# Two passes of 256 tokens over the last four output tiles of a two-layer encoder, with weights split once

## The chip, the cores and the metric

The kernel runs on one core of a Trainium2 chip. The metric is device time in microseconds (us) of one execution; less is better. Engines are named as in the profile: PE (TensorE, matrix products; PEld is its weight loads), DVE (VectorE), ACT (ScalarE), POOL (GpSimd) and SP (SyncE, whose queue issues most DMA transfers).

## The reference

The program computes a two-layer encoder trunk over 1024 tokens of width 1024: layer 0 with global, windowed and memory attention, layer 1 with neighbourhood and memory attention, each with a gate and an output projection that is added to the residual, and a last RMS norm. Cut to what the change touches, the end of layer 1 and the last norm:

```python
y = jnp.concatenate([yc, ym], axis=-1) * jax.nn.silu(gate)      # (1, 1024, 1536)
x = x + y @ w_out_odd[o]                                         # (1, 1024, 1024)
...
return rmsnorm(x, final_norm_gain)   # x * rsqrt(mean(x*x) + 1e-6) * gain, per token
```

## The kernel before

The transposed residual is held as eight tiles of 128 features by 1024 tokens. The output projection is done by Strassen's method in Winograd's form on halves: features (four tiles and four tiles), tokens (512 and 512) and the inner dimension (768 and 768), so seven groups of products in place of eight. The four quarters of the result are c11, c12, c21, c22, each of four tiles of 128 x 512: c12 and c22 are the first 512 tokens in the order of the norm, "the earlier half" below, and c11 and c21 are the second 512 tokens, the ones that are ready last.

Each product of a group is a tile of 128 features: six blocks of 128 inner rows, and for every block three PE products (high weights by high activations, high by low, low by high), since a 32-bit float is split in two parts for the array. So a tile is 18 PE products. Weights come as two units of 384 columns per tile: a transfer into a raw buffer (tile name wraw, four buffers), a rounding copy on ACT that gives the high part (wh), and a subtraction that gives the low part (wl), on DVE and POOL in turn. The raw buffer is free again after the subtraction.

The order of the groups at the end of layer 1 (`out_project`, called with `last=True`): after the other quarters, group a12 adds to c11 (four tiles, PE banks pj, pj, s, s), with the norm of the earlier half worked in between: column sums of squares (line 283), the root, transposes that spread the root over the partitions (line 133), and the scaling and transfers out (lines 1900 to 1903). A fence holds a12's fourth tile back behind these transposes. The last group, a22, adds to c21. Its activations are the six tiles named H, its four output tiles are named yb.

Group a22 before: tiles 0, 1 and 2 with 512 columns each, in the banks of a12; the weights of tile 3 are split, and `finish` takes over. It works tile 3 in two passes of 256 tokens: after each pass comes the difference (DVE), its square (ACT), the sum of squares as one-column products with a vector of 1/1024 (line 1473, PE, into `ss`), the root (line 1480 and DVE), transposes, and the scaling of all eight tiles for these 256 tokens by DVE and POOL, with four transfers of 256 KB for each 256 tokens. Squares of six of the eight tiles are added by POOL to one total (tile vt); two are summed by PE on their own.

The scheduler of the framework sets the order of the rest by its own model of times; `issue_after` and `Pinned` hold some instructions in a written order. The named lines: 242 and 1334 products, 283 and 1473 sums, 133 transposes, 1359 `plus`, 1364 and 1366 squares and their adding, 1281 low parts of weights, 1518 the square of a difference, 1499 and 1501 POOL's scaling, 1496 transfers out. Instructions that go through `Pinned` carry line 62, those of `copy` line 125.

Of the kernel before, what the change touches and what calls it, by code (L numbers as in the profile page):

```python
# [10 lines left out]
F32R = mybir.dt.float32r  # L11
I32 = mybir.dt.int32
AF = mybir.ActivationFunctionType
OP = mybir.AluOpType
# [10 lines left out]
UNIT = 4  # L25
# [39 lines left out]
class Trunk:  # L65
# [1246 lines left out]
    def out_project(self, w, sd, yd, res, done, tags, banks, first, begun, last=False):  # L1312
# [4 lines left out]
        nc = self.nc  # L1317
        xb, yb = banks
        cut = [slice(u * 384, u * 384 + 384) for u in range(2)]

        def weights(i, kind, us=(0, 1)):

            src = sd[i][:, "3124".index(kind[1]), :] if kind[0] == "s" else w[i if kind[1] == "1" else 4 + i][:, 768 * (kind[2] == "2"):]
            for c in (cut[u] for u in us):
                with self.ahead("w"):
                    raw = self.st("wraw", [128, UNIT * 128], pool=self.base, bufs=4)[:, :384]
                    nc.sync.dma_start(raw, src[:, c])
                    yield self.w_parts(raw, self.either())
# [40 lines left out]
        apart = 7  # L1369
        c11, c22, c12, c21 = (self.halves(t) for t in tags["c"])  # L1370
        at = lambda c, i: c[i // 2][:, i % 2, :]
# [11 lines left out]
        y = self.y_parts(yd, tags["y"][1], "t1")  # L1383
# [7 lines left out]
        y = self.y_parts(yd, tags["y"][2], "t2")  # L1391
# [42 lines left out]
                square(x, i)  # L1434

        y = self.y_parts(yd, tags["y"][6], "t4", after)
        apart = 6 if last else 7
        for i in range(4):
            x = at(c21, i)
            if last and i == 3:  # L1440
                ws = list(weights(3, "a22"))
                break
            product(y, xb[i], weights(i, "a22"), True)
            with self.ahead("sink"):
                plus(x, xb[i], OP.subtract)
                square(x, 4 + i)
        if not last:
            list(done(c11 + c21, sums, 512, 512))
            return
        self.finish(c11 + c21, sums, [product, y, ws], at(c21, 3))  # L1450

    def finish(self, xs, sums, last, x3):

        nc, tc = self.nc, self.tc
        pinned = Pinned(tc, nc.vector)
        product, y, ws = last
        gains = [self.gain[:, 24 + kt:25 + kt] for kt in range(KT)]  # L1460
        at = [xs[k // 2][:, k % 2, :] for k in range(KT)]
        for k in range(7):
            if k < 3:
                nc.gpsimd.tensor_scalar(at[k], at[k], gains[k], 1.0, op0=OP.mult, op1=OP.mult)
            else:
                self.copy(at[k], at[k], gains[k])
        sq = self.st(self.square_tag, [128, 512])
        ss, rows = [self.ps("pv")[:, :16] for _ in range(2)], {}

        def sum_up(h, parts, start):  # L1470
            for i, a in enumerate(parts):
                for b, c in enumerate(range(cols[h].start, cols[h].stop, 128)):
                    self.last = nc.tensor.matmul(ss[h][:, b:b + 1], a[:, c:c + 128], self.inv_d, start=start and i + b == 0,
                                                 stop=not start, skip_group_check=True)

        def root(h):
            n = 2
            t = ss[h][:, 8:8 + n]
            r, y = (self.st(k, [128, n], pool=self.base, bufs=2) for k in ("rq_v", "rq_y"))
            nc.scalar.activation(t, ss[h][:, :n], AF.Sqrt, bias=self.eps)  # L1480
            pinned.reciprocal(r, t)
            yield
            pinned.scalar_tensor_tensor(t, ss[h][:, :n], EPS, r, op0=OP.add, op1=OP.mult)
            yield
            pinned.scalar_tensor_tensor(t, t, -0.5, r, op0=OP.mult, op1=OP.mult)
            yield
            pinned.scalar_tensor_tensor(y, t, 1.5, r, op0=OP.add, op1=OP.mult)
            yield
            rows[h] = [self.rows_of(y, n, k) for k in ("tr", "pj")]

        def scale(h):
            c = cols[h]
            sb = self.st("vt", [128, 512])[:, :c.stop - c.start]
            self.copy(sb, rows[h][1])
            two = lambda t: t[:, None, :].to_broadcast([128, 2, c.stop - c.start])
            out = lambda p: nc.sync.dma_start(
                self.io["out"][2 * p:2 * p + 2, :, 512 + c.start:512 + c.stop].rearrange("k p t -> p k t"), xs[p][:, :, c])
            x = xs[0][:, :, c]
            nc.gpsimd.tensor_tensor(x, x, two(sb), op=OP.mult)
            if h == 0:  # L1500
                nc.gpsimd.tensor_tensor(at[2][:, c], at[2][:, c], sb, op=OP.mult)
            for p in (2, 3):
                x = xs[p][:, :, c]
                pinned.tensor_tensor(x, x, two(rows[h][0]), op=OP.mult)
                yield
                out(p)
            if h == 0:
                pinned.tensor_tensor(at[3][:, c], at[3][:, c], rows[h][0], op=OP.mult)
            else:
                x = xs[1][:, :, c]  # L1510
                pinned.tensor_tensor(x, x, two(rows[h][0]), op=OP.mult)
            yield
            out(0)
            out(1)

        def difference(p, c):
            pinned.tensor_tensor(x3[:, c], x3[:, c], p, op=OP.subtract)
            nc.scalar.activation(sq[:, c], x3[:, c], AF.Square)
            self.copy(x3[:, c], x3[:, c], gains[7])
        cols = [slice(0, 256), slice(256, 512)]  # L1520
        p = self.ps("pj")[:, :256]
        product(y, p, ws, True, cols[0])
        difference(p, cols[0])
        p = self.ps("pj")[:, :256]
        end = product(y, p, ws, True, cols[1], range(2))
        with tc.issue_after(end.ins):
            sum_up(0, sums, True)
        with tc.issue_after(self.last.ins):
            end = product(y, p, ws, True, cols[1], range(2, 3))
        with tc.issue_after(end.ins):  # L1530
            sum_up(0, [sq], False)
        with tc.issue_after(self.last.ins):
            end = product(y, p, ws, True, cols[1], range(3, 6))
            sum_up(1, sums, True)
        first = root(0)
        for _ in range(4):
            next(first)
        difference(p, cols[1])
        with tc.issue_after(end.ins):
            list(first)  # L1540
        with tc.issue_after(self.turned.ins):
            sum_up(1, [sq], False)
        one = scale(0)
        next(one)
        next(one)
        list(root(1))
        list(one)
        list(scale(1))

    def front(self, w, pairs, order, values, plan, x1, squares, dests):  # L1550

# [675 lines left out]
```

## Time and profile before

| | |
|---|---|
| median of 3 runs | 1487.39 us (1487.01 to 1491.83) |
| the profiled execution, time | 1488.39 us |
| its span, first to last instruction | 1486.6 us |
| PE busy | 1465.6 us, 99% of the span |
| DVE, ACT, POOL busy | 70%, 56%, 43% |
| mean granted PE clock | 0.998 |
| chain that ended last | PE 85%, DMA 5%, DVE 4%, all else 6% |

The rows give the start of an instruction and its duration, both in us from the start of the span. PE products are pipelined: the listed duration of one (0.28 to 0.4 us) is longer than the distance to the next start, so that the price of a product is read from the distance of starts. In PE's rows a sum or a product that is built of several passes counts each of them (a one-column sum is two rows of PE).

### The profile page before, as it was taken

Reading aid. Unit: us, or ns where it says so; the run is one execution under the profiler, and the core shown is the slowest. Engines: PE = TensorE matmul, PEld = TensorE weight load, DVE = VectorE, ACT = ScalarE, POOL = GpSimd, SP = SyncE. Lnnn points to the kernel's source line nnn. Section 1 sums busy time; section 2 is a strip of 40 time slices with the busy share of each in tenths; the row PEclk is TensorE's granted clock in tenths of the full one; section 3 lists DMA queues with packets and bytes.
Section 4 is the critical chain, followed back from the end, with each engine's and each line's share of the span. In section 5 each row is a group of like instructions: output and inputs, shape, how many; then the busy total and the mean of one; then the engine's idle time right before and its main releaser. Section 6 shows DMA issues by size and latency. Waiting matters only on the chain.

```text
span 1486.6 us, 25518 instructions
## 1 busy us (share of the span) xinstructions
PE 1465.6 (99%) x8433; PEld 1275.1 (86%) x8433; DVE 1034.8 (70%) x2124; ACT 837.9 (56%) x1877; POOL 642.2 (43%) x767
## 2 busy tenths in 40 slices
PE   9899999999999999999999999999999999999998
PEld 8798888988888788888879887888998888888886
DVE  6687777777776578776687776654446787778674
ACT  7743665556655366655444444444446777777454
POOL 1223568556765656553450000001425556664454
PEclk9999999999999999999999999999999999999999
DMA  8966334334343524378553343567665568788834
GB/s 286 306 159 183 118 119 162 114 128 137 115 139 106 172 76 141 106 265 310 185 181 128 128 140 136 157 169 245 229 245 173 187 195 272 235 287 316 315 107 144
DMA packets 173860, 271.92 MB, mean 183 GB/s; under 512 B 15648, under 2 KB 96800, under 8 KB 172704
## 3 DMA queue, kind: packets, MB, share of 16 engines
q1 hardware_dynamic: 173296, 270.20, 56.2%
q8 instruction: 67, 1.10, 0.3%
q14 instruction: 65, 0.53, 0.1%
q10 hardware_dynamic: 432, 0.09, 0.0%
HBM read 174.28 MB, written 83.89 MB: 174 GB/s over the span
## 4 chain that ended last, share of the span: by engine, by line
PE 85%; DMA 5%; DVE 4%; issue 2%; ACT 2%; POOL 2%; SPq 0%; POOLq 0%; DVEq 0%; ACTq 0%
PE pj L242 15%; PE pj L62 11%; PE x L1619 7%; PE tr L133 6%; PE pv L1068 4%; PE y L1619 4%; PE pv L62 3%; PE s L62 3%; PE pj L1334 3%; PE tr L62 3%; PE sa L1334 2%; PE pv L1619 2%; PE sa L1035 2%; PE sa L1036 2%; PE s L1334 2%
## 5 line engine op out<-in xcount | busy, mean ns | idle before, releaser
L542 DVE TENSOR_TENSOR pl<-tr,ph 128x512 fp32r<-128x512 f32 (+2 forms) x352 | 204.1, 594 | 45.0 <-ACT ph L125 43.0
L242 PE MATMUL pj<-H,wh 128*128 128x512 f32 x704 | 233.7, 412 | 0.5 <-DVE vt L313 0.2
L125 ACT ACTIVATE ph<-tr 128x512 fp32r<-128x512 f32 (+2 forms) x352 | 176.3, 522 | 100.5 <-PE tr L133 76.4
L158 POOL TENSOR_SCALAR wh<-wraw 128x512 fp32r<-128x512 f32 x48 | 32.6, 682 | 275.9 <-PE x L1619 234.0
L125 ACT ACTIVATE wh<-wraw 128x384 fp32r<-128x384 f32 (+1 forms) x163 | 89.0, 553 | 99.4 <-DMA wraw<-w_mem 12.9
L242 PE MATMUL pj<-H,wl 128*128 128x512 f32 x352 | 139.1, 395 | 0.0
L242 PEld LDWEIGHTS pj<-H,wh 128*128 128x128 f32 x704 | 120.2, 189 | 18.3 <-POOL wh L158 1.1
L62 PE MATMUL pj<-H,wh 128*128 128x512 f32 x384 | 121.0, 396 | 0.0
L1121 POOL TENSOR_SCALAR pn<-pn,st 128x384 f32<-128x384 f32 (+1 forms) x128 | 72.4, 567 | 104.7 <-DVE st L1120 69.0
L133 PE MATMUL tr<-ident,P 128*128 128x128 f32 x752 | 115.4, 273 | 0.7 <-DVE pl L542 0.4
L1281 POOL TENSOR_TENSOR wl<-wraw,wh 128x384 fp32r<-128x384 f32 x56 | 63.2, 1130 | 91.4 <-ACT wh L125 85.6
L1119 ACT ACTIVATE pn<-pn,st 128x384 f32<-128x384 f32 (+1 forms) x128 | 75.1, 587 | 42.2 <-DVE st L1116 41.0
L133 PEld LDWEIGHTS tr<-ident,P 128*128 128x128 f32 x752 | 88.9, 140 | 9.1 <-DVE pl L542 1.4
L1041 ACT ACTIVATE P<-sa,st 128x1024 f32<-128x1024 f32 x64 | 71.5, 1117 | 35.3 <-PE tr L133 19.1
L1043 POOL TENSOR_SCALAR P<-P,st 128x1024 f32<-128x1024 f32 x64 | 74.0, 1159 | 32.3 <-DVE st L1042 32.3
L1040 DVE TENSOR_REDUCE st<-sa 128x1 f32<-128x1024 f32 x64 | 77.5, 1219 | 8.3 <-PE sa L1036 7.9
L62 PE MATMUL s<-k,q 128*128 128x384 f32 (+1 forms) x352 | 81.2, 327 | 0.0
L242 PEld LDWEIGHTS pj<-H,wl 128*128 128x128 f32 x352 | 66.2, 188 | 15.3
L62 PE MATMUL pj<-H,wl 128*128 128x512 f32 x192 | 75.6, 394 | 0.0
L160 POOL TENSOR_TENSOR wl<-wraw,wh 128x512 fp32r<-128x512 f32 x52 | 68.7, 1324 | 10.9 <-ACT wh L125 8.4
L62 PEld LDWEIGHTS pj<-H,wh 128*128 128x128 f32 x384 | 66.6, 188 | 5.4
L853 PE MATMUL pj<-ah,H 128*128 128x256 f32 x384 | 70.5, 281 | 0.0
(569 smaller groups left out, 4187.1 us busy)
## 6 DMA issues: line engine op xcount, KB each, us to landing
wraw<-w_o SPq DMA_DIRECT2D x52, 256.0 KB, 4.1
y<-yb SPq DMA_DIRECT2D x24, 512.0 KB, 3.2
wraw<-s SPq DMA_DIRECT2D x64, 192.0 KB, 3.7
wraw<-w_e SPq DMA_DIRECT2D x44, 256.0 KB, 3.2
k<-k SPq DMA_DIRECT2D x42, 256.0 KB, 5.4
s<-bias SPq DMA_DIRECT2D x56, 192.0 KB, 2.0
wq<-w_o SPq DMA_DIRECT2D x40, 256.0 KB, 3.4
y<-sg SPq DMA_DIRECT2D x18, 512.0 KB, 3.3
```

What stands on the lines that cost most here:

```text
L62: return lambda *a, **k: self.tc.keep_in_program_order(getattr(self.engine, name)(*a, **k))
L125: return self.nc.scalar.activation(out, in_, AF.Copy, scale=scale)
L133: self.turned = self.fence = self.pe.transpose(o, i, self.ident)
L242: self.pe.matmul(a[:, :n], s[:, kt % UNIT, :], m, start=(kt == 0 and i == 0), stop=(kt == KT - 1 and i == 2))
L542: self.low = nc.vector.tensor_tensor(pl[:, :n], tr[:, :n], ph[:, :n], op=OP.subtract)
L1040: nc.vector.tensor_reduce(st[:, 0:1], s, axis=AX.X, op=OP.max, negate=True)
L1041: nc.scalar.activation(pt, s, AF.Exp, bias=st[:, 0:1], accum_out=st[:, 1:2])
L1043: self.normal = nc.gpsimd.tensor_scalar(pt, pt, st[:, 2:3], 0.5, op0=OP.mult, op1=OP.mult)
L1119: nc.scalar.activation(o, o, AF.Exp, bias=st[:, 0:1], scale=-1.0, accum_out=st[:, 2:3])
L1121: self.normal = normal = nc.gpsimd.tensor_scalar(o, o, st[:, 3:4], 0.5, op0=OP.mult, op1=OP.mult)
L1334: last = nc.tensor.matmul(bank, s[:, k, :], y[3 * u + k][m][:, cols], start=start and u + k + e == 0, stop=u == 1 and k + e == 4, skip_gro ...
L1619: self.last = nc.tensor.matmul(bank, ws[s][:, k, :], b[k][m], start=start and k + i == 0, stop=k == UNIT - 1 and i == 2, skip_group_check= ...
```

## The change

The last group a22 as a whole moves into `finish`. All four tiles are worked in two passes of 256 tokens: the first pass of all four goes into the banks named tr (two tiles to a bank), the second pass into the four banks of a12. The eight weight units are split once, into buffers of their own (names pn for the high part, ph and pl for the low part), and serve both passes. The sums, root, transposes, scaling and transfers of the first 256 tokens stand between the tiles of the second pass; the sums of the second 256 tokens stand ahead of the last six products. Two of the last four transfers are issued from ACT's queue.

```diff
         y = self.y_parts(yd, tags["y"][6], "t4", after)
-        apart = 6 if last else 7
+        if last:
+            self.finish(c11 + c21, sums[0], w[4:], y, product, xb, yb)
+            return
...
+        ws = []
+        for i in range(4):
+            parts = []
+            for u, tag in enumerate(("ph", "pl")):
+                with self.ahead("w"):
+                    raw = self.st("wraw", [128, UNIT * 128], pool=self.base, bufs=4)[:, :384]
+                    nc.sync.dma_start(raw, w[i][:, 768 + u * 384:1152 + u * 384])
+                    h, l = (self.st(t, [128, 3, 128], F32R) for t in ("pn", tag))
+                    hf, lf = (t.rearrange("p a b -> p (a b)") for t in (h, l))
+                    self.copy(hf, raw)
+                    self.either().tensor_tensor(lf, raw, hf, op=OP.subtract)
+                    parts.append((h, l))
+            ws.append(parts)
+
+        def difference(i, p, c):
+            x = at[4 + i][:, c]
+            pinned.tensor_tensor(x, x, p, op=OP.subtract)
...
+            nc.scalar.activation(sq, x, AF.Square)
+            self.copy(x, x, gains[4 + i])
+            if i < 2:
+                nc.gpsimd.tensor_tensor(total[:, c], total[:, c], sq, op=OP.add)
+            return sq
...
+            for p, e in ((2, pinned), (3, pinned), (0, nc.gpsimd), (1, pinned if h else nc.gpsimd)):
                 x = xs[p][:, :, c]
...
+                e.tensor_tensor(x, x, two(rows[0] if e is pinned else sb), op=OP.mult)
+                (nc.scalar if h and p % 2 else nc.sync).dma_start(
+                    self.io["out"][2 * p:2 * p + 2, :, 512 + c.start:512 + c.stop].rearrange("k p t -> p k t"), x)
+
+        first = []
+        for p in range(2):
+            for i in range(2):
+                product(y, yb[p][:, 256 * i:256 * i + 256], ws[2 * p + i], i == 0, cols[0])
+            for i in range(2):
+                first.append(difference(2 * p + i, yb[p][:, 256 * i:256 * i + 256], cols[0]))
+
+        def second(i):
+            p = xb[i][:, :256]
+            end = product(y, p, ws[i], True, cols[1])
+            return end, difference(i, p, cols[1])
+        end, _ = second(0)
         with tc.issue_after(end.ins):
-            sum_up(0, sums, True)
+            sum_up(0, total[:, cols[0]], True)
+            for i in (2, 3):
+                sum_up(0, first[i], stop=i == 3)
+        y0 = root(0)
         with tc.issue_after(self.last.ins):
-            end = product(y, p, ws, True, cols[1], range(2, 3))
+            end, _ = second(1)
         with tc.issue_after(end.ins):
-            sum_up(0, [sq], False)
+            scale(0, y0)
+        with tc.issue_after(self.turned.ins):
+            end, a = second(2)
+        p = xb[3][:, :256]
+        with tc.issue_after(end.ins):
+            end = product(y, p, ws[3], True, cols[1], range(4))
+        with tc.issue_after(end.ins):
+            sum_up(1, total[:, cols[1]], True)
+            sum_up(1, a)
         with tc.issue_after(self.last.ins):
-            end = product(y, p, ws, True, cols[1], range(3, 6))
-            sum_up(1, sums, True)
...
+            product(y, p, ws[3], True, cols[1], range(4, 6))
+        a = difference(3, p, cols[1])
+        sum_up(1, a, stop=True)
+        scale(1, root(1))
```

The order on PE around the end of a12's third tile (bank s_16425) and the norm's transposes (line 133), before:

```order
L1334 MATMUL s_16425<-q_17131,wh_17243 128x512 x2
L1334 MATMUL s_16425<-q_17131,wl_17244 128x512
L133 MATMUL tr_17265<-ident_63,iq_y_17224 128x128 x4
L1334 MATMUL s_16426<-k_17126,wh_17290 128x512 x2
L1334 MATMUL s_16426<-k_17126,wl_17291 128x512
```

The same place in the changed kernel, where 58 of the 64 products that now stand between are left out:

```order
L1334 MATMUL s_16425<-q_17131,wl_17244 128x512
L1334 MATMUL tr_16427<-H_17322,pn_17354 128x256 x2
...
L1334 MATMUL tr_16428<-H_17327,pl_17385 128x256
L1334 MATMUL tr_16428<-H_17322,pn_17390 128x256 x2
...
L1334 MATMUL tr_16428<-H_17325,pn_17396 128x256
L133 MATMUL tr_17265<-ident_63,iq_y_17224 128x128 x4
L1334 MATMUL s_16426<-k_17126,wh_17290 128x512 x2
```

The first three tiles of the first pass and ten products of the fourth now stand between a12's third tile and the transposes; a12's fourth tile stays behind the transposes.

The end of PE's order, from the last products (bank pj_17491) on, before (pv is `ss`, vt the total of squares, bm the squares that are summed on their own):

```order
L1334 MATMUL pj_17491<-H_17327,wl_17456 128x256
L1473 MATMUL pv_17468<-inv_d_67,vt_17181 128x1 x2
L1473 MATMUL pv_17468<-inv_d_67,bm_17445 128x1 x2
L133 MATMUL tr_17530<-ident_63,rq_y_17521 128x128 x2
L133 MATMUL pj_17533<-ident_63,rq_y_17521 128x128 x2
L1473 MATMUL pv_17468<-inv_d_67,bm_17466 128x1 x2
L133 MATMUL tr_17552<-ident_63,rq_y_17546 128x128 x2
```

The end of PE's order in the changed kernel, from the products ahead of the last six:

```order
L1334 MATMUL s_16426<-H_17325,pl_17397 128x256
L1492 MATMUL pv_17347<-inv_d_67,vt_17181 128x1 x2
L1492 MATMUL pv_17347<-inv_d_67,bt_17581 128x1 x2
L1334 MATMUL s_16426<-H_17326,pn_17396 128x256 x2
L1334 MATMUL s_16426<-H_17326,pl_17397 128x256
L1334 MATMUL s_16426<-H_17327,pn_17396 128x256 x2
L1334 MATMUL s_16426<-H_17327,pl_17397 128x256
L1492 MATMUL pv_17347<-inv_d_67,bt_17581 128x1 x2
L133 MATMUL tr_17618<-ident_63,rq_y_17612 128x128 x2
```

Four sums of the second 256 tokens and the four transposes of the first stood behind the last product; now they stand ahead of it (the transposes between the second and third tile of the second pass, not shown).

The end of POOL's order in the changed kernel, from the scaling of the earlier half (line 1903) on; before, line 1366 added squares of 512 columns in these places:

```order
L1903 TENSOR_TENSOR mk_16435<-mk_16435,vt_17270 128x512 x2
L1366 TENSOR_TENSOR vt_17181<-vt_17181,bm_17319 128x512
L1487 TENSOR_TENSOR vt_17181<-vt_17181,bm_17437 128x256 x2
L1487 TENSOR_TENSOR vt_17181<-vt_17181,bm_17507 128x256 x2
L1514 TENSOR_TENSOR H_16431<-H_16431,vt_17552 128x2x256
```

The total that PE sums is complete for the first 256 tokens only after POOL's add for a12's fourth tile and two adds more.

## Rows read from the trace of the kernel before

**Rows 1.** Stages: window, its length, each engine's busy time (instructions), granted clock, DMA share, GB/s.

```profile
1471.00:1477.00 6.00, 6.00 (x54) 5.96 (x52) 1.85 (x7) 2.52 (x5) 0.00 (x0) 1.00 0.01 3
1477.00:1480.00 3.00, 1.51 (x15) 1.42 (x14) 2.26 (x8) 1.37 (x4) 1.31 (x2) 0.95 0.11 39
1480.00:1487.00 7.00, 1.09 (x4) 0.71 (x4) 2.16 (x4) 0.38 (x1) 1.90 (x2) 0.50 0.80 283
```

**Rows 2.** The chain that ended last: start, duration, engine, tile, line, instructions.

```profile
1439.71 8.37 PE pj L1334 x36
```

**Rows 3.** PE in order of time: start, duration, line, operation, shapes, count.

```profile
1453.89 0.60 PE L133 MATMUL tr<-ident,iq_y 128*128 128x128 f32 x4
...
1471.12 0.40 PE L1334 MATMUL pj<-H,wh 128*128 128x256 f32 x2
...
1473.97 0.50 PE L1473 MATMUL pv<-inv_d,vt 128*128 128x1 f32 x4
...
1476.73 0.50 PE L1473 MATMUL pv<-inv_d,vt 128*128 128x1 f32 x4
...
1477.54 0.41 PE L133 MATMUL tr<-ident,rq_y 128*128 128x128 f32 x2
...
1478.01 0.50 PE L1473 MATMUL pv<-inv_d,bm 128*128 128x1 f32 x4
```

**Rows 4.** All engines in order of time; brackets: idle before, and who ended it.

```profile
1456.48 2.72 DVE L1902 SCALAR_TENSOR_TENSOR H<-H,gain,tr 128x512 f32<-128x512 f32 x4
...
1475.76 0.24 ACT L1480 ACTIVATE pv<-pv,eps 128x2 f32<-128x2 f32 x1 [0.83 <-PE pv L1473]
...
1476.03 0.17 DVE L62 RECIPROCAL rq_v<-pv 128x2 f32<-128x2 f32 x1 [2.15 <-ACT pv L1480]
...
1477.99 1.28 DVE L62 TENSOR_TENSOR yb<-yb,tr 128x512 f32<-128x512 f32 x2 [0.64 <-PE tr L133]
...
1478.55 0.24 ACT L1480 ACTIVATE pv<-pv,eps 128x2 f32<-128x2 f32 x1
...
1479.19 0.16 DVE L62 RECIPROCAL rq_v<-pv 128x2 f32<-128x2 f32 x1
...
1480.10 0.66 PE L133 MATMUL tr<-ident,rq_y 128*128 128x128 f32 x2 [1.59 <-DVE rq_y L62]
...
1481.68 1.26 POOL L1499 TENSOR_TENSOR H<-H,vt 128x512 f32<-128x512 f32 x1 [1.05 <-ACT vt L125]
...
1482.71 0.92 SPq L1496 DMA_DIRECT2D out<-H  x2
```

**Rows 5.** Groups by line and shape, 1440 to 1487: busy time, mean ns, idle before.

```profile
L1366 POOL TENSOR_TENSOR vt<-vt,bm 128x512 f32<-128x512 f32 x6 | 7.8, 1296 | 0.8 <-ACT bm L1364 0.6
L1281 POOL TENSOR_TENSOR wl<-wraw,wh 128x384 fp32r<-128x384 f32 x7 | 7.7, 1105 | 9.2 <-ACT wh L125 9.2
...
L125 ACT ACTIVATE yb<-yb,gain 128x256 f32<-128x256 f32 x2 | 1.0, 509 | 0.1
...
L125 ACT ACTIVATE H<-H,gain 128x512 f32<-128x512 f32 x1 | 0.7, 724 | 0.0
L1501 POOL TENSOR_TENSOR H<-H,vt 128x256 f32<-128x256 f32 x1 | 0.7, 722 | 0.0
```

**Rows 6.** DMA issues: weights (1425 to 1490), first and last transfer out of the tail.

```profile
wraw<-w_oo SPq DMA_DIRECT2D x16, 192.0 KB, 2.4
...
out<-yb SPq DMA_DIRECT2D x1, 256.0 KB, 2.1
...
out<-H SPq DMA_DIRECT2D x1, 256.0 KB, 2.5
```

**Rows 7.** SP's queue in order of time, 1449.5 to 1450.

```profile
1449.56 0.33 SPq L1327 DMA_DIRECT2D wraw<-w_oo  x1
```

**Rows 8.** The page's DMA issues: size of one, median us from issue to landing.

```profile
k<-k SPq DMA_DIRECT2D x42, 256.0 KB, 5.4
```

**Rows 9.** PE's waits over the whole span: total us, times, longest.

```profile
PE tr L133 <- POOL rp L887: 1.6, 1, 1.6
```

More of the change, by code (lines that the diff above doesn't have):

```diff
@@ L1436, in out_project @@
         y = self.y_parts(yd, tags["y"][6], "t4", after)
-        apart = 6 if last else 7
+        if last:
+            self.finish(c11 + c21, sums[0], w[4:], y, product, xb, yb)
+            return
         for i in range(4):
             x = at(c21, i)
-            if last and i == 3:
-                ws = list(weights(3, "a22"))
-                break
             product(y, xb[i], weights(i, "a22"), True)
@@ L1446, in out_project, with finish @@
                 square(x, 4 + i)
[L1447 to L1452, printed above, removed]
+        list(done(c11 + c21, sums, 512, 512))
+    def finish(self, xs, total, w, y, product, xb, yb):
         nc, tc = self.nc, self.tc
         pinned = Pinned(tc, nc.vector)
-        product, y, ws = last
         gains = [self.gain[:, 24 + kt:25 + kt] for kt in range(KT)]
         at = [xs[k // 2][:, k % 2, :] for k in range(KT)]
-        for k in range(7):
+        cols = [slice(0, 256), slice(256, 512)]
+        ss, rows = [self.ps("pv")[:, :16] for _ in range(2)], {}
+        for k in range(4):
             if k < 3:
@@ L1466, in finish, with sum_up @@
                 self.copy(at[k], at[k], gains[k])
[L1467 to L1474, printed above, removed]
+        ws = []
[14 more added lines that the diff above has]
+            pinned.tensor_tensor(x, x, p, op=OP.subtract)
+            if i % 2 == 0:
+                self.sq = self.st(("bm", "bt")[i // 2], [128, 512])
+            sq = self.sq[:, 256 * (i % 2):256 * (i % 2) + 256]
+            nc.scalar.activation(sq, x, AF.Square)
[3 more added lines that the diff above has]
+            return sq
+        def sum_up(h, a, start=False, stop=False):
+            for b in range(2):
+                self.last = nc.tensor.matmul(ss[h][:, b:b + 1], a[:, b * 128:b * 128 + 128], self.inv_d, start=start and b == 0,
+                                             stop=stop, skip_group_check=True)
         def root(h):
@@ L1481, in root, with scale @@
             pinned.reciprocal(r, t)
-            yield
             pinned.scalar_tensor_tensor(t, ss[h][:, :n], EPS, r, op0=OP.add, op1=OP.mult)
-            yield
             pinned.scalar_tensor_tensor(t, t, -0.5, r, op0=OP.mult, op1=OP.mult)
-            yield
             pinned.scalar_tensor_tensor(y, t, 1.5, r, op0=OP.add, op1=OP.mult)
-            yield
-            rows[h] = [self.rows_of(y, n, k) for k in ("tr", "pj")]
-        def scale(h):
+            return y
+        def scale(h, y):
+            rows = [self.rows_of(y, 2, "tr") for _ in range(2)]
@@ L1492, in scale @@
             c = cols[h]
[L1493 to L1501, printed above, removed]
@@ L1502, in scale @@
-            for p in (2, 3):
-                x = xs[p][:, :, c]
[L1504 to L1525, printed above, removed]
+            sb = self.st("vt", [128, 512])[:, :256]
+            self.copy(sb, rows[1])
+            two = lambda t: t[:, None, :].to_broadcast([128, 2, 256])
+            for p, e in ((2, pinned), (3, pinned), (0, nc.gpsimd), (1, pinned if h else nc.gpsimd)):
+                x = xs[p][:, :, c]
+                e.tensor_tensor(x, x, two(rows[0] if e is pinned else sb), op=OP.mult)
+                (nc.scalar if h and p % 2 else nc.sync).dma_start(
+                    self.io["out"][2 * p:2 * p + 2, :, 512 + c.start:512 + c.stop].rearrange("k p t -> p k t"), x)
@@ L1528, in finish @@
+        y0 = root(0)
         with tc.issue_after(self.last.ins):
-            end = product(y, p, ws, True, cols[1], range(2, 3))
+            end, _ = second(1)
         with tc.issue_after(end.ins):
-            sum_up(0, [sq], False)
-        with tc.issue_after(self.last.ins):
-            end = product(y, p, ws, True, cols[1], range(3, 6))
-            sum_up(1, sums, True)
[L1535 to L1548, printed above, removed]
+            scale(0, y0)
[7 more added lines that the diff above has]
+            sum_up(1, a)
```

## The prediction

> **What bounds the kernel now.** I read the page's busy times first: TensorE (PE) is busy 99% of the span, so nothing in the middle of the program can shrink unless PE gets less to do, and this change leaves it every column. The last stages [rows 1] show where time without PE work stands: none until 1477, then half of 3 us, then all but 1.09 of 7 us. So the change can act in two places: on when PE's last product ends (its last row starts at 1476.6), and on the tail of 9.7 us from there to the end of the span (difference from 1476.93, square, sum, root, transposes, scaling, transfers). I then read PE's rows for the price of each kind of product, the rows of the other engines in the tail, and the chain on DVE, ACT and POOL that must be through when PE wants to sum squares.
>
> **The change part by part.**
>
> *Narrower products.* Three tiles of 18 products with 512 columns become 108 products with 256. 36 wide ones take 8.37 us, 0.2325 each [rows 2]; 24 narrow ones start between 1471.12 and 1473.97, 0.1188 each [rows 3]. 54 x (2 x 0.1188 - 0.2325) = +0.27 us. Every product has its own weight load in both versions, and the measured spacing contains it.
> The Trainium skill (TensorE: Matmul & The Clock Gate, section Back-to-back issue gap) gives 81 ns at 128 columns and 131 ns at 512 for streams of load and product, so narrow ones are dear there. With a straight line between the two, my estimate from that page is 98 ns at 256, so 54 x (2 x 98 - 131) = +3.5 us instead of +0.27, and the run would end near 1493.3. The trace has both widths and disagrees with the page at 512 columns (232 ns), so the rows stand.
>
> *Sums and transposes that now come ahead of the last product.* Before, four one-column sums of the second half (1476.73 to 1477.54, 0.81 us) and the four transposes of the first half's roots (1477.54 to 1478.01, 0.47 us) run behind the last product [rows 3], while DVE and ACT make its difference and square. They are free there: the last sum has nothing to read before 1478. In the new order all of them stand ahead of the last six products of the last tile, so that cover is gone and PE's last product ends 1.28 us later.
>
> *A new wait for the total of squares.* In the new order 64 narrow products of the first pass (three tiles and ten products) go ahead of the transposes of the earlier half's norm, which PE runs at 1453.89 now [rows 3]. These move by 64 x 0.1188 = 7.60 us, to 1461.49, and behind them, at a fence, the fourth a12 tile. PE asks for the first sum after the first tile of the second pass: 1461.49 + 0.47 + 18 x 0.2325 + 8 x 0.1188 + 18 x 0.1188 = 1469.24. What the sum needs: DVE's products with the transposed rows, which end at 1456.48 + 2.72 = 1459.20 [rows 4], move by the same 7.60 to 1466.80; then DVE adds the fourth a12 tile (0.7), ACT squares it (0.6), POOL adds the square to the total (1.30), and after that makes two adds of 256 columns; the nearest POOL row of that width is a product with 0.72 [rows 5]. With 0.1 at each of three hand-overs the total is there at 1471.15, and PE waits 1.9 us. The ends: 1.25, if the narrow adds cost half of the 384-column row (1.1 us [rows 5]) and the hand-overs nothing; 2.8 if POOL's three adds take a third more. I take 1.9, by the nearest rows.
>
> *A second, smaller wait.* ACT has one gain of 512 columns, five of 256 and one square ahead of the first half's square root: from the end of the first pass's squares, 1469.9, on, 0.72 + 5 x 0.51 [rows 5] + 0.42 put the root at 1473.6. The reciprocal follows 0.27 later (1475.76 to 1476.03) and the transposes 0.91 after the reciprocal (1479.19 to 1480.10) [rows 4]: 1474.8. PE has six sums (1.2) and the second tile (2.14) behind 1471.15 and is there at 1474.5. 0.25 us, with 0 and 0.6 as ends.
>
> *The tail.* Its steps stay, but three things go. DVE's two products for the first half, 1.28 us from 1477.99, no longer stand ahead of the second reciprocal: that came 0.64 us after its root (1478.55 to 1479.19), where the first half's came after 0.27 [rows 4]: -0.37. The last four transfers come from two queues instead of one: SP's last two issues take 0.92 from 1482.71, and the second of them began near 1483.2, 0.2 after POOL's product was done at 1481.68 + 1.26 = 1482.94 [rows 4]: -0.2. And they meet an idle DMA: the last transfer landed after 2.5 us, the first of the eight after 2.1 [rows 6]: -0.4. Together -1.0, with -0.6 if landing doesn't improve. What is late next is POOL's product behind ACT's copy of the rows, which DVE's three products don't outlast; both are as long as before.
>
> *What costs nothing.* The eight weight units cost the same loads and splits, only earlier. The fourth load is issued at 1449.56 [rows 7], lands after 2.4 us [rows 6], is split in 0.5 (ACT) and 1.1 (POOL) [rows 5], and only then the eighth can go into its buffer: 1449.56 + 2.4 + 0.5 + 1.1 + 2.4 + 0.5 = 1456.5. PE asks for the eighth at 1453.89 + 63 x 0.1188 = 1461.4, so 4.9 us of cover. The outputs of the earlier half leave 7.6 us later and are still out ten us ahead of the last ones.
>
> **The sum:** +0.27 + 1.28 + 1.9 + 0.25 - 1.0 = +2.7 us. The profiled execution took 1488.39 us, so its like would take 1491.1; the median of the runs, 1487.39, lies 1.0 below that execution, and the forecast is 1490.1. Low end: the waits at 1.25 and 0, +0.27 + 1.28 + 1.25 - 1.0 = +1.8. High end: both waits at their upper ends and the smaller gain, +0.27 + 1.28 + 2.8 + 0.6 - 0.6 = +4.35. Its own range is 1489.2 to 1491.7. A measurement of this kernel can tell about 0.3% (4.5 us) from no change; the sum stays under that.
>
> **Rivals.**
>
> *The transfers set the end.* In the last stage DMA is busy 0.80 of 7 us and moves 283 GB/s on average [rows 1], so 354 GB/s while it is busy, or 0.74 us for one of the eight transfers of 256 KB, which follow each other closely. If this queue and not the data set the end, four fewer would take 3.0 us off the tail instead of 1.0: +0.27 + 1.28 + 2.15 - 3.0 = +0.7, 1488.1. Against it: the last transfer landed only 0.4 us later than the first [rows 6], and its data was ready 0.2 us before it was issued [rows 4].
>
> *Weights late in the first pass (the slower side).* PE now takes a unit each 9 x 0.1188 = 1.07 us, where it took one each 2.1; supply through four raw buffers is 2.4 + 0.5 + 1.1 = 4.0 us for four, so just as fast, and only the lead covers it. The eighth unit contains two landings, so it decides from 2.4 + 4.9 / 2 = 4.85 us of landing on. At 5.4, the median that the page has for another load [rows 8], PE stands 2 x 3.0 - 4.9 = 1.1 us in the first pass: 1491.2, slower than before. At 6 us it would be 1492.4. Against it: sixteen loads of this very kind have the median of 2.4 [rows 6].
>
> *The clock.* The granted clock was 1.00 until 1477, 0.95 in the next stage and 0.50 in the last [rows 1], once PE had run dry. If the new wait in the second pass made it fall to the lower level (1.2 GHz instead of 2.4), the 54 narrow products behind it would cost up to 54 x 0.119 = 6.4 us more: 1496.5, clearly slower. Against it: the wait stands between dense stretches of products, PE waited up to 1.6 us elsewhere [rows 9], and the page's row of clocks has 9 tenths or more in every slice. For it: 1.9 is longer than any of those waits.
>
> **How the numbers follow.** Forecast 0.66, transfers 0.14, weights late 0.06, clock 0.07, and 0.07 for the scatter of runs (two of the three shown lie 0.4 us apart, the third 4.4 above). Slower by over 0.3% (above 1491.85) take the clock's chance, a part of the weights' and a little of the scatter and of the forecast's upper end: 0.11. Faster by over 0.3% (under 1482.9) would need 7 us off the forecast, and no piece of the tail that the change touches is so long: 0.02. Within 0.3%: 0.87. The range runs from 1487.2, under the transfers case, to 1492.4, the weights case at 6 us.
>
> **What would show it.** Right: PE runs without a gap through 64 narrow products from about 1453.9; it waits once some 1.9 us for POOL's total near 1469 and a little on the root near 1474.5; its last product starts near 1480.3, 3.7 later than before; the second reciprocal comes 0.3 us after its root; the last difference is 8.7 us ahead of the end of the span instead of 9.7. Wrong: a PE wait on a weight split in the first pass; a clock under 1.00 before PE's last product; a tail under 7.5 us, by which the transfers were the answer; a last product at its old time, by which the moved sums would have cost nothing.

## The result and the profile after

The changed kernel takes 1492.43 us (median of 21 runs) against 1488.2 of the kernel before (21 runs), a ratio of 1.0032 with a 95% interval of 1.0021 to 1.0042. One of the changed kernel's 21 executions took 8272 us and is left out of the ratio; the median of the other 20 is 1492.2. The direction of the forecast (1490.1) was right; the size was not: +4.2 us (+4.0 by the 20) where the sum gave +2.7, just outside the range (its upper end is 1492.4) by the first median and just inside it by the second. The profiled execution took 1490.9 us with a span of 1489.1.

Two executions differ by some microseconds long before the change: PE starts a12's third tile, the last piece of work that stands alike in both, at 1449.62 before and at 1447.21 after. I therefore measure each trace from that row to the end of its span and call this the closing stretch. PE in order of time, the kernel before:

```profile
1449.62 0.71 PE L1334 MATMUL s<-k,wh 128*128 128x512 f32 x2
```

To the end of the span (1486.6) that is 36.98 us. The same engine in the changed kernel (start, duration, line, tile and inputs, shape, count; in brackets the idle time before and who ended it):

```profile
1447.21 0.71 PE L1334 MATMUL s<-k,wh 128*128 128x512 f32 x2
...
1451.48 0.40 PE L1334 MATMUL tr<-H,pn 128*128 128x256 f32 x2
...
1459.02 0.28 PE L1334 MATMUL tr<-H,pn 128*128 128x256 f32 x1
1459.14 0.60 PE L133 MATMUL tr<-ident,iq_y 128*128 128x128 f32 x4
...
1466.75 0.28 PE L1334 MATMUL pj<-H,pl 128*128 128x256 f32 x1
1468.87 0.61 PE L1492 MATMUL pv<-inv_d,vt 128*128 128x1 f32 x4 [1.83 <-POOL vt L1487]
1469.33 1.03 PE L1492 MATMUL pv<-inv_d,bt 128*128 128x1 f32 x8
1470.23 0.48 PE L1334 MATMUL pj<-H,pn 128*128 128x256 f32 x2
...
1472.36 0.63 PE L1334 MATMUL pj<-H,pn 128*128 128x256 f32 x2
...
1473.00 1.05 PE L133 MATMUL tr<-ident,rq_y 128*128 128x128 f32 x4
...
1478.03 0.50 PE L1492 MATMUL pv<-inv_d,vt 128*128 128x1 f32 x4
...
1479.52 0.28 PE L1334 MATMUL s<-H,pl 128*128 128x256 f32 x1
```

From 1447.21 to 1489.1 are 41.89 us, 4.91 more than before. The first part went as forecast: 64 narrow products without a gap from 1451.48, then the norm's transposes, 11.93 us into the stretch where they stood at 4.27 [rows 3]; one wait for POOL's total. The last product's row starts 32.31 us into the stretch, before at 26.99 (1476.61): 5.32 later, of which the tail gives back 0.41.

New is what follows the wait. Stages of the changed kernel (window, length, busy time of PE, PEld, DVE, ACT, POOL, granted clock, DMA share, GB/s), to be read beside [rows 1]:

```profile
1451.00:1466.50 15.50, 15.50 (x112) 14.59 (x111) 9.93 (x18) 4.85 (x12) 8.93 (x10) 1.00 0.37 134
1466.50:1471.50 5.00, 3.17 (x28) 2.96 (x27) 1.09 (x5) 3.75 (x10) 2.88 (x4) 1.00 0.31 119
1471.50:1475.50 4.00, 4.00 (x23) 4.00 (x22) 1.71 (x3) 1.18 (x3) 1.25 (x2) 0.57 0.04 14
1475.50:1480.00 4.50, 4.30 (x37) 4.09 (x35) 0.59 (x2) 0.93 (x2) 1.99 (x2) 1.00 0.63 221
```

In the second line PE is idle for 1.83 us; in the third it is busy all the time, at a granted clock of 0.57: for 3.4 of these 4 us the clock stands at the lower of its two levels (1.2 GHz instead of 2.4), and the products come about every 0.21 us instead of every 0.119 (three in 0.64 us from 1472.36 to 1473.00). "Busy" hides this; the clock column and the distance of starts show it. The fall does not come with the wait: PE's products start again at 1470.23, come every 0.119 us at first, and slow down from about 1471.6 on. Before, PE's products behind 1471 ran at 1.00 [rows 1].

The chain that PE waits for, on DVE, ACT and POOL of the changed kernel:

```profile
1460.40 1.41 DVE L1905 SCALAR_TENSOR_TENSOR sg<-sg,gain,tr 128x512 f32<-128x512 f32 x2 [3.67 <-ACT vt L125]
...
1461.73 2.71 DVE L1905 SCALAR_TENSOR_TENSOR H<-H,gain,tr 128x512 f32<-128x512 f32 x4
...
1464.36 0.68 DVE L1359 TENSOR_TENSOR H<-H,s 128x512 f32<-128x512 f32 x1
...
1465.13 0.63 ACT L1364 ACTIVATE bm<-H 128x512 f32<-128x512 f32 x1 [4.76 <-DVE H L1359]
...
1465.91 1.29 POOL L1366 TENSOR_TENSOR vt<-vt,bm 128x512 f32<-128x512 f32 x1 [2.90 <-ACT bm L1364]
...
1467.28 1.53 POOL L1487 TENSOR_TENSOR vt<-vt,bm 128x256 f32<-128x256 f32 x2
```

Read downwards, each step begins where the one above ends; DVE's products with the norm's rows end 7.6 us later, counted from the stretch's start, than in [rows 4], and everything below follows. The tail of the changed kernel, beside [rows 4]:

```profile
1479.83 0.42 DVE L62 TENSOR_TENSOR yb<-yb,s 128x256 f32<-128x256 f32 x1 [2.62 <-PE s L1334]
...
1481.40 0.24 ACT L1499 ACTIVATE pv<-pv,eps 128x2 f32<-128x2 f32 x1 [0.15 <-PE pv L1492]
1481.67 0.17 DVE L62 RECIPROCAL rq_v<-pv 128x2 f32<-128x2 f32 x1 [1.41 <-ACT pv L1499]
...
1484.17 1.27 POOL L1514 TENSOR_TENSOR H<-H,vt 128x512 f32<-128x512 f32 x1 [6.67 <-ACT vt L125]
...
1485.46 0.37 SPq L1515 DMA_DIRECT2D out<-H  x1
```

The reciprocal comes 0.27 after its root, as forecast (0.64 before). But from the end of POOL's last product to the end of the span are 3.66 us (1485.44 to 1489.1), and before just as many (1482.94 to 1486.6).

### The profile page after: what moved, and what is told of

Read it like the earlier page. It is cut to its first block, busy times and chain, and to the rows that moved or that the text cites. A ratio compares the mean times of both kernels' runs of the same rounds, so it can differ in the third digit from the quotient of the medians.

```text
span 1489.1 us, 25626 instructions
## 1 busy us (share of the span) xinstructions
PE 1468.4 (99%) x8487; PEld 1279.9 (86%) x8487; DVE 1034.8 (69%) x2126; ACT 839.1 (56%) x1883; POOL 646.0 (43%) x769
## 4 chain that ended last, share of the span: by engine, by line
PE 81%; DMA 7%; DVE 4%; POOL 3%; issue 3%; ACT 2%; SPq 0%; POOLq 0%; DVEq 0%; ACTq 0%
PE pj L242 14%; PE pj L62 12%; PE x L1622 7%; PE tr L133 5%; PE y L1622 4%; PE pv L62 3%; PE s L62 3%; PE pv L1068 3%; PE tr L62 3%; PE sa L1334 2%; PE pv L1622 2%; PE pj L1334 2%; PE tr L1334 2%; PE sa L1035 2%; PE sa L1036 2%
## 5 line engine op out<-in xcount | busy, mean ns | idle before, releaser
L125 ACT ACTIVATE wh<-wraw 128x384 fp32r<-128x384 f32 (+1 forms) x155 | 84.5, 555 | 90.3 <-PE tr L1347 10.7
L1281 POOL TENSOR_TENSOR wl<-wraw,wh 128x384 fp32r<-128x384 f32 x52 | 58.2, 1121 | 89.8 <-ACT wh L125 71.3
```

The source lines that it names most:

```text
L125: return self.nc.scalar.activation(out, in_, AF.Copy, scale=scale)
```

## The experiments

The theory after the two traces: the late norm makes PE wait 1.83 us, this lets the clock fall behind it, and both are on the path. The rivals: the clock fell for another reason, or the added sums explain the loss. Ratios and medians are against the kernel before, run beside each experiment; a closing stretch is read from one trace. How far the median of a kernel lies above that of the kernel before and how far its closing stretch does agree within 0.7 us, except in e5_pe (+4.55 by medians, +5.87 by stretch) and in e4_sp (+6.14 and +4.61).

**New banks for the first pass (e1_bank).** The norm's transposes need a bank named tr, of which there are two, and in the changed kernel both stay with `finish` until the first pass is through with them.

```
+        yb = [self.ps("tr") for _ in range(2)]
```

> Edit: finish takes two new banks named tr for its first pass, instead of the two that group a22 was handed; nothing else. In the compiled order the earlier half's norm transposes then stand behind 9 narrow products instead of 64. Measure: the stretch from the start of a12's third tile to the end of the span, 36.98 us in the kernel before, 41.89 in the changed one. Theory (the late norm chain makes PE wait 1.83 us, and behind this wait the granted clock falls to half for some 3.7 us, which costs 1.8 to 1.9 more): the transposes start near 5.2 us after the stretch's start instead of 11.9, the wait for POOL's total is gone, a shorter one on ACT's squares of the third and fourth tile (0.3 to 0.8 us) may take its place, the clock stays at 1.00 until the last product; the stretch takes 38.2 to 39.0 us and the run is 3 to 3.7 us faster than the changed kernel. Rival 1 (the wait costs its own length and the clock falls for another reason, such as the one-column sums): 40.0 to 40.5, the clock still falls. Rival 2 (the waits are covered and the added work of sums and transposes is all): no change from 41.9.

Measured: 1490.4 us median (ratio 1.0017, 1.0004 to 1.003), closing stretch 39.92 us, 1.97 less. The wait for the first half's total is gone and the clock keeps 1.00 up to the last product, so rival 2 falls, and so does rival 1's falling clock, though 39.92 lies nearer to its number than to the theory's. But it is 0.9 more than the theory's upper end, and the squares of the third and fourth tile were not waited for. A wait that nobody expected took the place: PE for the norm itself. The stage from the first half's sums to the last product, and all engines around the norm:

```profile
1470.00:1479.30 9.30, 9.09 (x76) 8.79 (x75) 2.97 (x9) 3.86 (x10) 3.99 (x4) 1.00 0.32 113
...
1453.21 1.97 POOL L1475 TENSOR_TENSOR pl<-wraw,pn 128x384 fp32r<-128x384 f32 x2
...
1453.29 0.96 DVE L784 SCALAR_TENSOR_TENSOR iq_t<-iq_t,rq_v 128x4 f32<-128x4 f32 x1
...
1454.28 0.92 DVE L785 SCALAR_TENSOR_TENSOR iq_y<-iq_t,iq_y 128x4 f32<-128x4 f32 x1
...
1455.25 0.65 PE L133 MATMUL tr<-ident,iq_y 128*128 128x128 f32 x4 [0.98 <-DVE iq_y L785]
```

Two DVE steps of 4 columns take 0.96 and 0.92 us; in the kernel before they take 0.17 and 0.16:

```profile
1451.56 0.17 DVE L784 SCALAR_TENSOR_TENSOR iq_t<-iq_t,rq_v 128x4 f32<-128x4 f32 x1
1451.75 0.16 DVE L785 SCALAR_TENSOR_TENSOR iq_y<-iq_t,iq_y 128x4 f32<-128x4 f32 x1
```

**The wait filled (e2_fill).** PE gets 15 products more, with operands that are at hand, in the place of its idle time:

```
+            end = product(y, xb[3][:, :256], ws[0], True, cols[1], range(5))
+        with tc.issue_after(end.ins):
             sum_up(0, total[:, cols[0]], True)
```

> Edit: the changed kernel, with 15 further narrow products (weights and activations that are at hand, into the bank that the fourth tile of the second pass starts afresh) where PE waits for POOL's total; their result is overwritten. The wait of 1.83 us is filled with 15 x 0.119 = 1.79 us of products, so nothing but PE's idleness changes. Theory (the idle stretch lets the clock fall): the clock stays at 1.00 through the second pass, the 256-column spacing stays 0.119 us there; the stretch from a12's third tile to the end takes 40.0 us instead of 41.89, 1.8 to 1.9 us less, although PE has more to do. Rival (the clock falls for another reason, the one-column sums or the power of the whole kernel): 41.9 or more, with the half rate from the same place on.

Measured: 1490.52 us (ratio 1.002, 1.0007 to 1.0033), closing stretch 40.54. The last product's row starts at 30.78 instead of 32.31. PE does 15 products more and is 1.53 us earlier, though its sums start at the same place (21.69 us into the stretch, 21.66 in the changed kernel):

```profile
1470.00:1474.00 4.00, 3.94 (x34) 3.74 (x34) 0.63 (x3) 3.31 (x9) 2.47 (x4) 1.00 0.28 105
1474.00:1479.00 5.00, 5.00 (x45) 5.00 (x44) 2.49 (x7) 1.32 (x4) 2.25 (x3) 1.00 0.27 96
```

The second stage is the one that ran at the lower clock in the changed kernel; here it has 1.00. So leaving PE without products there is a cause of the fall, and the fall costs 1.5 us beside the wait. The 1.5 us rest on the two traces; the medians lie +3.4 above the kernel before here and +4.2 for the changed kernel, with intervals that overlap. The theory's 40.0 was 0.5 too low.

**The second half's sums behind the last product (e3_sums).**

```
-            end = product(y, p, ws[3], True, cols[1], range(4))
+            end = product(y, p, ws[3], True, cols[1])
```

(and the last six products behind the sums go).

> Edit: the changed kernel, with the four one-column sums of the second half's total and third tile behind the last product again, instead of ahead of its last six. Theory (their 0.81 us lies on the path where they stand now, and behind the last product they run beside DVE's difference and ACT's square, 0.93 us): the stretch from a12's third tile to the end takes 41.1 us instead of 41.89; the wait and the fallen clock stay as they are. Rival (they fill a gap that opens anyway, or are late for the last sum behind them): 41.9 or more.

Measured: 1490.91 us (ratio 1.0019, 1.0004 to 1.0034), closing stretch 40.67, 1.22 less, where 0.8 was expected. The wait of 1.83 and the fallen clock are there as before. The last product's row comes 0.93 earlier (31.38); the rest is the last transposes, which took 0.62 us here and 1.09 in the changed kernel's trace, at the lower clock.

**Less for POOL, more sums for PE (e5_pe).**

```
-            if i < 2:
+            if i < 2 and c.start:
                 nc.gpsimd.tensor_tensor(total[:, c], total[:, c], sq, op=OP.add)
...
-            for i in (2, 3):
+            for i in range(4):
```

> Edit: the changed kernel, with the first half's squares of the first two tiles summed by PE on their own (four more one-column sums) instead of added to the total by POOL (two adds, 1.53 us). The total is then ready some 1.5 us sooner. Theory (the length of PE's idle time sets whether the clock falls): the wait shrinks from 1.83 to 0.3 us, four sums add 0.46, the clock stays at 1.00: the stretch from a12's third tile to the end takes 41.89 - 1.5 + 0.46 - 1.9 = 39.0 us. Rival (the clock falls over the one-column sums and not over the wait, so more of them don't help): 40.8 us, with the half rate still there.

Measured: 1491.66 us (ratio 1.0027, 1.0015 to 1.004), closing stretch 42.85, a microsecond more than the changed kernel. Both numbers failed; of the rival the fallen clock came true. The wait did shrink to 0.22, and the clock fell all the same, for longer:

```profile
1470.00:1472.00 2.00, 1.78 (x17) 1.60 (x15) 0.42 (x1) 2.00 (x6) 0.35 (x1) 1.00 0.56 213
1472.00:1478.50 6.50, 6.50 (x33) 6.50 (x33) 1.74 (x7) 1.54 (x5) 0.72 (x1) 0.51 0.01 4
```

Before it fell, PE had made nothing but one-column sums since 1470.40, shown as busy. So the length of the idle time in the profile's sense does not decide.

**The wait alone, apart from most of the sums (e7_apart).** Nine products between the sums of the total and the others:

```
             sum_up(0, total[:, cols[0]], True)
+        with tc.issue_after(self.last.ins):
+            end = product(y, xb[3][:, :256], ws[0], True, cols[1], range(3))
+        with tc.issue_after(end.ins):
             for i in (2, 3):
```

> Edit: the changed kernel, with 9 further narrow products (overwritten later) between the sums of the total, for which PE waits 1.83 us, and the four sums of the third and fourth tile's squares. The wait stays; the stretch in which PE has no products is cut from 3.5 us (1.83 idle, 1.4 of one-column sums, the way in and out) into two of 2.3 and 1.0. Theory (what lets the clock fall is the whole stretch without products, one-column sums included): the clock stays at 1.00 and the stretch from a12's third tile to the end takes 41.89 - 1.76 + 1.07 + 0.1 = 41.3 us. Rival (the idle time of 1.83 us alone does it): the clock falls again and it takes 42.9 us or more.

Measured: 1494.4 us (ratio 1.0047, 1.0029 to 1.0064), closing stretch 44.72. The theory in this form falls; the wait with two sums behind it, 2.5 us without a product (1468.80 to 1471.29), was followed by a fall, and the clock was at its lower level for six microseconds:

```profile
1468.80:1470.60 1.80, 0.00 (x1) 0.00 (x0) 0.42 (x1) 1.80 (x5) 1.62 (x3) 1.00 0.54 205
1470.60:1471.00 0.40, 0.37 (x3) 0.37 (x3) 0.00 (x0) 0.40 (x2) 0.00 (x0) 0.88 0.07 26
1471.00:1477.00 6.00, 6.00 (x30) 6.00 (x30) 0.67 (x4) 1.02 (x3) 0.73 (x1) 0.50 0.01 2
```

**One queue for the last transfers (e4_sp).**

```
-                (nc.scalar if h and p % 2 else nc.sync).dma_start(
+                nc.sync.dma_start(
```

> Edit: the changed kernel, with the last two transfers of the second half issued from SP like the others, not from ACT's queue. Theory (the second queue is worth the 0.2 us of the prediction): from the last product to the end 9.8 us instead of 9.58, the stretch from a12's third tile to the end 42.1 instead of 41.89. Rival (the transfers of ACT's queue land later, 2.4 us against 2.1, and take back what the second queue gives): 9.4 to 9.6, no loss.

Measured: 1493.19 us (5 runs; ratio 1.0042, 1.0029 to 1.0055), closing stretch 41.59. From the last transposes to the end are 6.26 us, with transposes of 0.62; the kernels that use both queues and have transposes of 0.62 take 6.22 (e3_sums) and 6.26 (e7_apart). From the last product to the end are 9.32 us, the same as in e7_apart with both queues. The second queue is worth nothing that these traces can tell. The rival's "no loss" held; the median of five runs is too uncertain to add to this, and whether a later landing on ACT's queue is the reason was not shown.

**New banks and late sums together (e6_two),** the two diffs above.

> Edit: two edits together, the new banks for the first pass (which alone gave 39.92 us for the stretch from a12's third tile to the end, against 41.89) and the second half's sums behind the last product (alone 40.67). Theory (they act in different places, the first on the wait and the clock, the second on the end): 41.89 - 1.97 - 1.22 = 38.7 us, clock 1.00 until the last product. Rival (the second one's gain came from the clock's return, not from the place of the sums): 39.5 or more.

Measured: 1488.71 us (ratio 1.0002, 0.999 to 1.0013), closing stretch 39.05. The gains add up but for 0.35. On PE they add up in full: the last product comes 2.91 earlier than in the changed kernel (29.40 into the stretch), where the two alone give 1.96 and 0.93, although the norm's wait is longer (1.40, 0.98 with the new banks alone). The 0.35 lies in the tail, 9.65 us from the last product's row against 9.29 in e3_sums: the last transposes took 1.09 here and 0.62 there.

**The weights' copies later (e8_late).** On top of e6_two:

```
-                    self.copy(hf, raw)
+                    with tc.issue_after(self.rooted.ins) if i else nullcontext():
+                        self.copy(hf, raw)
...
-        end, _ = second(0)
+        with tc.issue_after(end.ins):
+            end, _ = second(0)
```

(`rooted` is ACT's square root of the norm).

> Edit: e6_two, with ACT's copies of the weights of tiles 1 to 3 behind the square root of the earlier half's norm, and the second pass of tile 0 behind the whole first pass. With the new banks alone PE waited 0.98 us for this norm's last DVE step: ACT had two of these copies ahead of its table load, and two DVE steps of 128x4 took 0.96 and 0.92 us there where they took 0.17 and 0.16 before, while POOL made two of the weights' low parts. Theory (the splits, which the prediction took to be free, hold up this norm): the wait of 0.98 goes or falls under 0.3; the stretch from a12's third tile to the end takes 37.7 us where e6_two is expected at 38.7, and the run is within 1 us of the kernel before (36.98). Rival (the DVE steps are slow whatever ACT does, or the weights come late): 38.5 us or more.

Measured: 1489.95 us (ratio 1.0022, 1.0011 to 1.0033), closing stretch 39.40. The norm's transposes start earlier (6.20 us into the stretch, 6.90 in e6_two), but no products stand ahead of them now, so that the wait grew to 1.76. The two DVE steps still took 0.95 and 0.92, beside POOL's low parts, and a low part of DVE's own (0.94) stood ahead of them. The rival held, and it left POOL as the suspect.

This kernel also answers what a wait alone does. PE stood 1.76 us, with transposes and products right behind, and the clock stayed at 1.00 up to the last product:

```profile
1460.10 0.65 PE L133 MATMUL tr<-ident,iq_y 128*128 128x128 f32 x4 [1.76 <-DVE iq_y L785]
...
1454.00:1483.70 29.70, 27.94 (x200) 25.99 (x200) 14.12 (x29) 13.96 (x30) 17.65 (x18) 1.00 0.38 134
```

**No low parts on POOL (e9_dve).** On top of e6_two:

```
-                    self.either().tensor_tensor(lf, raw, hf, op=OP.subtract)
+                    nc.vector.tensor_tensor(lf, raw, hf, op=OP.subtract)
```

> Edit: e6_two, with all eight low parts of the last group's weights made by DVE instead of DVE and POOL in turn. In e6_two PE waited 1.40 us for the earlier half's norm (stretch from a12's third tile to the end 39.05 us); in e8_late, with fewer copies ahead of this norm, it waited 1.76, and both had two DVE steps of 128x4 at 0.95 and 0.92 us where the kernel before has 0.17 and 0.16, each time while POOL was making low parts. Theory (POOL's low parts slow DVE's small steps beside them): the two steps take 0.2 each again, PE's wait of 1.40 goes, the stretch takes 37.6 us. Rival (the steps are slow for another reason, such as ACT's copies or the loads): the steps stay above 0.8, the wait stays, 39 us or more since DVE has more to do.

Measured: 1486.11 us against 1486.61 (ratio 0.9996, 0.9983 to 1.001), closing stretch 37.07, 0.5 under the theory's number, with last transposes of 0.62 (1.09 in e6_two). DVE has four low parts more to do and is through earlier:

```profile
1457.05 0.16 DVE L784 SCALAR_TENSOR_TENSOR iq_t<-iq_t,rq_v 128x4 f32<-128x4 f32 x1
1457.24 0.16 DVE L785 SCALAR_TENSOR_TENSOR iq_y<-iq_t,iq_y 128x4 f32<-128x4 f32 x1
```

The wait is gone. The Trainium skill (SBUF — State Buffer, section Who interferes with whom) has the rule: a DVE instruction with two inputs in SBUF and a GpSimd instruction that reads SBUF contend, since DVE's second input comes through the read interface that the two share, and only one of them can hold it at a time. These runs agree: the two steps, with two inputs each, take 0.92 to 0.97 us beside POOL's low parts (1.0 each), 0.16 without them.

**Both (e10_both).** e9_dve, with the copies and low parts of tiles 1 to 3 held behind the norm's root and the second pass behind the first.

> Edit: e9_dve, with ACT's copies of the weights of tiles 1 to 3 behind the square root of the earlier half's norm, DVE's low parts of these behind its last step, and the second pass of tile 0 behind the whole first pass. Theory: the norm's transposes run 4.3 us after the start of a12's third tile without a wait, as in the kernel before, and nothing else changes against e9_dve: 37.4 to 37.7 us for the stretch, which is 0.27 for the narrower products and 0.47 for the moved transposes above the kernel before (36.98), less some 0.3 of tail; the median within 1 us of the kernel before. Rival (weights that are split later come late for the first pass): a PE wait on a low part and 38.5 us or more.

Measured: 1486.55 us against 1486.61 (ratio 1.0, 0.999 to 1.001), closing stretch 37.44. PE runs the norm's transposes 4.27 us into the stretch, as before, and the last product 27.80 into it:

```profile
1452.33 0.60 PE L133 MATMUL tr<-ident,iq_y 128*128 128x128 f32 x4
...
1475.86 0.28 PE L1334 MATMUL s<-H,pl 128*128 128x256 f32 x1
```

That is 0.81 later than in the kernel before, where 0.27 for narrower products and 0.47 for moved transposes were expected. The tail gives back 0.35. Against e9_dve the last product is where it was (27.77 there); the 0.37 more in the stretch are the last transposes, 1.09 here and 0.62 there. With the waits on the norm and on the total removed, and the second half's sums behind the last product again, the change is worth nothing: the stretch is 0.46 longer in these two traces, the medians are alike. No version here is measurably faster than the kernel before.

The mean granted clock of single runs points the same way without a trace. At 0.998 or above were 4 of the 55 runs of the five kernels whose traces show the fall in the second pass (1 of 20 of the changed one, 3 of 12 in e3_sums, none in e4_sp, e5_pe and e7_apart), and 49 of the 71 of the six whose traces don't (e1_bank 6 of 12, e2_fill 7, e8_late 6, e9_dve 10, e10_both 12, e6_two 8 of 11); of the kernel before, run beside the first four experiments, 24 of 35. It is a coarse sign, since the mean holds every stage: e8_late and e9_dve have another fall near 1330 us, behind a wait of over 3 us, and e2_fill one near 227 us, in work that the change leaves alone.

## Why the prediction was wrong, point by point

*Narrower products, +0.27.* Right as far as it was measured: together with the 0.47 of the moved transposes it makes 0.74, and e10_both is 0.81 later. The two were not measured apart.

*Sums and transposes ahead of the last product, +1.28.* Right in kind: moving the sums back gave 0.93 on PE, against 0.81 (the two products right behind the sums take some 0.08 more than others).

*The wait for the total, +1.9.* Right: 1.83, by the chain that was forecast. Its cause was told too narrowly: the transposes stood behind the first pass because both banks named tr were taken; with new banks they were early without any other edit.

*The second wait, +0.25.* Wrong by its whole size: it did not occur, in the changed kernel, where the slow products in front of it gave it time, nor with the wait filled, at full clock. ACT's root began at 1470.40, 23.2 us into the closing stretch; the prediction's 1473.6 is 24.0 into it. The prediction took each of ACT's gains at its listed 0.51 us, but one after another they start 0.40 apart (four from 1467.51 to 1469.10), and ACT was through 0.36 before PE's sums: the root waited for these.

*The clock, rival with a chance of 0.07.* This is the step that failed: the sum put the clock behind the wait at nothing. "Against it: the wait stands between dense stretches of products, PE waited up to 1.6 us elsewhere" holds for a wait alone, as the 1.76 us of e8_late show, but the prediction left out that six one-column sums follow this wait: 1.83 us idle and 1.36 us of sums, with no product in between. The clock fell, but only for a part of the second pass: +1.53 by e2_fill, where the rival's price was up to 6.4. The sum had neither. With it, the sum would have been +4.2, the difference of the medians; that this fits is in part luck, since the tail's gain was forecast 0.6 too large and the second wait 0.25, and the two traces differ by 4.91.

*The tail, −1.0.* It measured −0.41 (9.58 us from the last product's row to the end, before 9.99). The reciprocal's 0.37 is there. This term was 0.6 too large: the 0.2 for two queues and the 0.4 for landing are not there: 3.66 us from POOL's last product to the end in both traces, and one queue does as well as two.

*What costs nothing.* Wrong in one respect, though it cost nothing in the changed kernel, where the two steps took 0.97 and 0.95 but the transposes stood 64 products back: the weights' low parts on POOL hold up the norm on DVE, 0.98 to 1.76 us as soon as the norm is on the path. And the cover of the last weight unit was about 1.8 us, not 4.9: ACT copied it at 1456.77, after 3.68 us of waiting for its load, and PE took it at 1459.02.

The terms as measured: 0.27 + 0.93 + 0.47 + 1.83 + 1.53 − 0.41 = +4.62 of 4.91 us. The remaining 0.3 is not assigned; the ways from products to sums and back are one candidate.

## What to carry to other kernels

A wait on the matrix engine is not priced by its length alone: look at what stands between the last product ahead of it and the first behind it, ask whether the clock outlives that, put that price into the sum and not only among the rivals, and look at the clock of the stage behind the wait. A handed-on bank orders work as surely as a fence does: before moving work into a bank, look for who else is due there. Small two-input steps on DVE that sit on the path should not have POOL's two-input work beside them.

## What the runs showed of the hardware that was not expected

- In e5_pe the clock fell to 0.51 for 6.5 us after a wait of only 0.22 and one-column sums alone since then, shown as busy. Ahead of the falls in the second pass PE had run no product for 3.2 us (the changed kernel), 3.0 (e5_pe) and 2.5 (e7_apart); where it had run none for 1.4 us (e2_fill) or 2.2 (e8_late, transposes included), the clock stayed at 1.00. That length alone does not decide: behind the last product of all, the clock fell after 2.2 us in the changed kernel and after 5.2 in e3_sums, with one-column sums in between and in e3_sums the last transposes too. What decides was not settled.
- How long the clock stays down differs: 3.4 us in the changed kernel, some 6.5 in e5_pe and e7_apart. And it may not fall in every run: 3 of 12 runs of e3_sums, which has the wait, had a mean clock of 0.998 or above.
- The four last transposes take 0.62 or 1.09 us in one and the same place, by the clock at that moment, and move the end by 0.3 us.
